# An encoder layer on one core: x^T from a second host layout, and the mean square by products with ones

## The chip, the core and the metric

The kernel runs on one core of a Trainium2 chip. The metric is the device time in microseconds (us) of one execution; the median of three runs is taken. The core's engines work side by side, each through its own list of instructions in order: TensorE (PE, matrix products into PSUM; PEld are its weight loads), VectorE (DVE), ScalarE (ACT), GpSimd (POOL) and SyncE (SP), which issues the DMA transfers. They wait for each other by semaphores.

## The reference

One layer of an encoder with 256 tokens and 2048 features, in float32. What bears on the change is the first norm and the first projections:

```python
def rms_norm(x, w):
    y = xf * lax.rsqrt(jnp.mean(xf * xf, axis=-1, keepdims=True) + EPS)
    return y * w
h = rms_norm(x, norm_mix_pre[l])
proj = jnp.einsum('bsd,dc->bsc', h, w_in[l])      # 2048 -> 10240 columns
qa, ka, va, qn, kn, vn, gates = jnp.split(proj, split_at, axis=-1)
```

Then follow two attention branches (qa and ka with rotary embedding), sigmoid gates, an output projection with post-norm and residual, and an MLP with 8192 hidden features.

## The kernel before

All 256 tokens are handled at once. Every product is made from operands in two float32r parts (high and low, whose sum is the float32 value). Weights come in chunks of four 128-row tiles by 512 columns (1 MB), each by one load on SP's queue; ACT casts the high part (line 115) and DVE subtracts it for the low part (line 116). Raw, high and low chunks have three buffers each. A group `wgroup` makes 512 output columns: 16 tiles k of the contraction in four chunks, four blocks b of 128 columns, each in its own PSUM bank, and per (b, k) a pair of products: the high weights on 512 columns (line 191: high and low part of the activations) and the low weights on 256 (line 192). The first group, qa_p, goes k by k in its first chunk and block by block in the others. Then come ka_p and, by `agroup`, va_p.

The activations hT are x^T times the gain g_pre, in two parts. x is loaded in four blocks of 512 features for all tokens (the first in two halves, with the first chunk's weights, one load per k, between them). `x_parts(i)` transposes block i on PE, two transposes per k (line 268), ACT takes the high part out of PSUM (line 273) and DVE the low part (line 274). `prelude(ch)` is traced ahead of chunk ch: x_parts(0) and (1) at chunk 0, (2) and (3) at chunks 1 and 2; the squares x_squares(0) at chunk 2, (1) to (3) at chunk 3.

The norm's scale is applied behind the products. `x_squares` squares on ACT and accumulates per token (line 345). `postlude`, traced in the last chunk behind block 0, calls `row_scales`: a reduction on DVE (line 300), then (mean + eps)^-0.5 with POOL's power (line 88), then `along_tokens`, which spreads the scale over all partitions by products with a tile of ones (rxb_p, line 78), and the multiplication of the cosine and sine tables by it (lines 304, 305). The rotary step of the evacuation of qa_p needs these tables, but the PSUM banks come free before it.

The order on each engine is planned by a list scheduler from the order in which the instructions are traced and from a simulated timeline; `issue_after` adds single constraints. The same x is loaded again for the residual, much later.

Of the kernel before, what the change touches and what calls it, by code (L numbers as in the profile page):

```python
# [11 lines left out]
F32 = mybir.dt.float32  # L12
F32R = mybir.dt.float32r
AF = mybir.ActivationFunctionType
ALU = mybir.AluOpType
# [23 lines left out]
def encoder_layer(ctx: ExitStack, tc: tile.TileContext, a, out):  # L39
# [32 lines left out]
    def along_tokens(r, b, name):  # L72
        """r [P tokens, token tile] as a row of all tokens, on all partitions."""
        ps = bank(f"{name}_p")
        for t in range(2):
            dg = t1k(f"{name}_d{t}")
            nc.vector.tensor_scalar_mul(dg[:, :P], ident, r[:, t : t + 1])
            nc.tensor.matmul(ps[:, t * P : (t + 1) * P], ones, dg[:, :P], start=True, stop=True)
        nc.scalar.copy(b, ps[:, :T])

    def inv_rms(ss, n, name, r=None):
        """(ss / n + eps) ** -0.5, per partition."""
        w = ss.shape[1]
        ms_ = small(w, f"{name}_m")
        nc.vector.tensor_scalar(ms_, ss, 1.0 / n, EPS, op0=ALU.mult, op1=ALU.add)  # L85
        if r is None:
            r = small(w, f"{name}_r")
        nc.gpsimd.tensor_tensor(r, ms_, expo[:, :w], op=ALU.pow)
        return r

# [1 line left out]
    last_load = [None]  # L92

    def load(src, k0, nk, c0, cw, name):
        """Rows k0*128.. of a weight: [P, nk, cw]."""
        raw = wp.tile([P, nk, cw], F32, tag="raw", name=f"{name}_w")
        view = src[k0 * P : (k0 + nk) * P, c0 : c0 + cw].rearrange("(k p) c -> p k c", p=P)
        last_load[0] = nc.sync.dma_start(raw, view).ins
        return raw

    def split(raw, name, pieces=2, after=()):
        """Two float32r parts whose sum is raw. after[s] are instructions that go ahead of piece s."""
        _, nk, cw = raw.shape
        hi = wp.tile([P, nk, cw], F32R, tag="hi", name=f"{name}_h")
        lo = wp.tile([P, nk, cw], F32R, tag="lo", name=f"{name}_l")
        for s in range(pieces):
            part = (
                (slice(None), slice(s * nk // pieces, (s + 1) * nk // pieces))
                if nk > 1
                else (slice(None), slice(None), slice(s * cw // pieces, (s + 1) * cw // pieces))  # L110
            )
            with ExitStack() as order:
                for ins in after[s] if after else ():
                    order.enter_context(tc.issue_after(ins))
                nc.scalar.copy(hi[part], raw[part])  # L115
                nc.vector.tensor_sub(lo[part], raw[part], hi[part].bitcast(F32))  # L116
        return hi, lo
# [3 lines left out]

# [1 line left out]
    g_pre = const.tile([P, KD], F32, name="g_pre")  # L123
# [6 lines left out]
    nc.gpsimd.memset(ones, 1.0)  # L130
    x = a["x"]
    xv = x.rearrange("(t p) c -> p t c", p=P)
    xp = []
    first = []
    for i in range(4):
        xt = page([P, 2, 512], F32, f"x_{i}")
        xi = xv[:, :, i * 512 : (i + 1) * 512]
        xp.append(xt)
        if i == 0:
            raw = wp.tile([P, 4, 512], F32, tag="raw", name="first0_w")  # L140
            view = a["w_in"][: 4 * P, QA : QA + 512].rearrange("(k p) c -> p k c", p=P)
            for h in range(2):
                cs = slice(h * 256, (h + 1) * 256)
                nc.sync.dma_start(xt[:, :, cs], xi[:, :, cs])
                for k in range(h * 2, h * 2 + 2):
                    nc.sync.dma_start(raw[:, k], view[:, k])
            first.append(raw)
        else:
            nc.sync.dma_start(xt, xi)
            if i < 3:  # L150
                first.append(load(a["w_in"], i * 4, 4, QA, 512, f"first{i}"))
    g_mlp = const.tile([P, KD], F32, name="g_mlp")
# [19 lines left out]
    def advance(n):  # L172
        """Trace the next n stages of the attention heads that wait for their turn, and one chore."""
        if chores:
            with tc.issue_after(last_load[0]):
                chores.pop(0)()
        for _ in range(n):
            if pending:
                g = pending.pop(0)
                if next(g, None):  # L180
                    pending.append(g)

    def wgroup(src, c0, act, nk, evac, name, first=(), hook=None, mid=None, after={}, k_first=False, inner=None):
        """out^T of 512 columns: weights stationary. act(k) is [P, hi 256 | lo 256]."""
        ps = [bank(f"{name}_p{b}", True) for b in range(4)]
# [34 lines left out]
    def agroup(src, c0, stat, nk, evac, name, tail=1, between=None):  # L220
        """out of 512 columns: activations stationary. stat(k, t) is (hi, lo) of [P, 128].
        The last ``tail`` chunks go token tile by token tile; between(i) may trace instructions
        ahead of the i-th of the second tile's products there and returns the last of them."""
        ps = [bank(f"{name}_p{t}", True) for t in range(2)]
# [26 lines left out]
    def halves(ps, name):  # L251
        """The sum of the two halves of a bank, in SBUF."""
        r = t1k(f"{name}_r")
# [4 lines left out]

# [1 line left out]
    hT = [page([P, 2, 512], F32R, f"hT{i}") for i in range(8)]  # L260

    def x_parts(i):
        """The transpose of four tiles of x times the gain, in two parts [P, hi | lo]."""
        acts = []
        for k in range(i * 4, i * 4 + 4):
            pt = bank(f"hT_t{k}")
            for t in range(2):
                nc.tensor.transpose(
                    pt[:, t * P : (t + 1) * P], xp[i][:, t, (k % 4) * P : (k % 4 + 1) * P], ident
                )  # L270
            d = hT[k // 2][:, k % 2]
            g = g_pre[:, k : k + 1]
            acts.append(nc.scalar.activation(d[:, :T], pt[:, :T], AF.Copy, scale=g).ins)
            nc.vector.scalar_tensor_tensor(
                d[:, T:], pt[:, :T], g, d[:, :T].bitcast(F32), op0=ALU.mult, op1=ALU.subtract
            )

        return acts
# [16 lines left out]

    ssx = const.tile([P, 8], F32, name="ssx")

    def row_scales():
        sx = small(2, "sx")
        nc.vector.tensor_reduce(sx, ssx.rearrange("p (t h) -> p t h", h=4), axis=AX.X, op=ALU.add)  # L300
        inv_rms(sx, D, "rx", rx)
        along_tokens(rx, rxb, "rxb")
# [16 lines left out]

    # Position bias: row (h, i) of rpbp holds the bias of row offset i - 3 at column offsets  # L320
    # -63..63. Each is written 64 times at a pitch of 127 and read at a pitch of 126.
    def skew_write(h):
# [18 lines left out]

    def x_squares(i):
        for t in range(2):
            j = junk512("jx0").rearrange("p a b -> p (a b)")
            nc.scalar.activation(
                j, xp[i][:, t], AF.Square, accum_out=ssx[:, t * 4 + i : t * 4 + i + 1]
            )

    def postlude():
# [15 lines left out]

# [1 line left out]
    oT = {}  # L367
# [6 lines left out]
    def product3(ps, stat, s_at, mov, m_at, start, stop):  # L374
        """ps (+)= stat^T @ mov, each given in two parts."""
        for i, (sp, mp) in enumerate(((0, 0), (0, 1), (1, 0))):
# [42 lines left out]
    def p_transposed(p, name):  # L419
        """[P queries, (t, keys)] -> [P keys, (key tile, queries)]"""  # L420
        pt = bank(f"{name}_pt")
# [171 lines left out]

# [1 line left out]
    mT = []  # L595
# [26 lines left out]

# [1 line left out]
    def mstat(k, t):  # L624
# [9 lines left out]
    for t in range(2):  # L634
        for h in range(2):
            nc.sync.dma_start(
                x2[t * 2 + h], x[t * P : (t + 1) * P, h * 1024 : (h + 1) * 1024]
            )
# [77 lines left out]

# [1 line left out]
    def first_up_inner(k):  # L718
# [103 lines left out]
def _host_arrays(inputs):  # L822
    f = {k: np.ascontiguousarray(v) for k, v in inputs.items()}
    arr = {
        "x": f["x"][0],
        "w_in": f["w_in"][0],
        "w_branch_a": f["w_branch_a"][0],
# [12 lines left out]
        "lam_k2": f["lam_k2"],  # L840
        # row offsets -3..3 are the ones that four rows reach
        "rpbp": np.pad(f["na_rpb"][0][:, 4:11], ((0, 0), (0, 0), (48, 48))),
# [30 lines left out]
```

## Time and profile before

| what | us |
|---|---|
| median of three runs | 1397.35 |
| lowest and highest run | 1396.53, 1397.74 |
| span of the profiled execution | 1394.5 |
| PE busy | 1374.6 |
| DVE busy | 835.8 |
| ACT busy | 668.7 |

The profiled execution is one run of the same program, from its first to its last instruction; a run's time holds some 3 us around that. Line numbers are those of the kernel before. In a timeline row stand the start, the duration and, in brackets, how long the engine had been idle and what ended that; "x4" merges four instructions that follow each other. Matmul ends are modelled, so the distance between starts tells the pace. A float32 product or transpose counts as one or two matmul rows.

### The profile page before, as it was taken

What the parts mean: (1) busy time and instruction counts of PE and PEld (TensorE: products, weight loads), DVE (VectorE), ACT (ScalarE), POOL (GpSimd) and SP (SyncE); (2) the same over time, 40 slices, a digit from 0 to 9 for tenths busy, and PEclk for the clock granted to TensorE, in tenths of its full rate; (3) what the DMA queues carried; (4) which work ended last, traced back from release to release, by engine and by line L of the source; (5) the groups of instructions that cost most, each with busy time, mean ns of one, the idle gap of its engine ahead of it and who ended that gap; (6) DMA issues with size and microseconds to landing.
All of it is one profiled execution on the core that took longest, in us unless ns stands there. A gap on an engine that the chain in (4) does not pass through costs nothing.

```text
span 1394.5 us, 17896 instructions
## 1 busy us (share of the span) xinstructions
PE 1374.6 (99%) x7240; PEld 1177.8 (84%) x7240; DVE 835.8 (60%) x1155; ACT 668.7 (48%) x1023; POOL 7.9 (1%) x19
## 2 busy tenths in 40 slices
PE   7999999999999999999899999999999999999997
PEld 6888888888888888888788888888888888888886
DVE  6868866676656565654755555555575554444445
ACT  7554554545444445543744444444464543334332
POOL 0000000000000000000000000000000000000000
PEclk9999999999999999999999999999999999999999
DMA  9674755564555555675455565656555556555551
GB/s 317 202 214 154 202 177 173 171 191 155 165 205 182 203 181 183 203 279 184 149 182 181 182 193 170 211 170 200 189 196 185 203 186 227 195 187 205 181 199 73
DMA packets 117490, 265.16 MB, mean 190 GB/s; under 512 B 15008, under 2 KB 16288, under 8 KB 109216
## 3 DMA queue, kind: packets, MB, share of 16 engines
q1 hardware_dynamic: 117264, 264.03, 57.3%
q8 instruction: 56, 0.92, 0.3%
q14 instruction: 26, 0.21, 0.0%
q10 hardware_dynamic: 144, 0.01, 0.0%
HBM read 261.92 MB, written 3.92 MB: 191 GB/s over the span
## 4 chain that ended last, share of the span: by engine, by line
PE 98%; DVE 1%; DMA 0%; ACT 0%; SPq 0%; issue 0%; DVEq 0%; POOLq 0%; POOL 0%; ACTq 0%
PE u_p L191 17%; PE u_p L192 9%; PE acc L779 8%; PE acc L778 8%; PE acc L777 8%; PE gb_p L191 4%; PE ga_p L191 4%; PE qa_p L191 2%; PE gb_p L192 2%; PE ga_p L192 2%; PE ka_p L191 2%; PE qn_p L191 2%; PE bb_p L191 2%; PE ba_p L191 2%; PE kn_p L191 2%; PE y_p L229 2%
## 5 line engine op out<-in xcount | busy, mean ns | idle before, releaser
L191 PE MATMUL u_p<-h2T,u_h 128*128 128x512 f32 x1024 | 359.9, 398 | 0.5 <-DVE r_m L85 0.5
L192 PE MATMUL u_p<-h2T,u_l 128*128 128x256 f32 x1024 | 284.3, 280 | 0.0
L116 DVE TENSOR_TENSOR d_l<-d_w,d_h 128x1024 fp32r<-128x1024 f32 x128 | 151.1, 1221 | 164.2 <-ACT d_h L115 163.7
L116 DVE TENSOR_TENSOR u_l<-u_w,u_h 128x1024 fp32r<-128x1024 f32 x128 | 151.1, 1222 | 146.0 <-ACT u_h L115 144.7
L191 PEld LDWEIGHTS u_p<-h2T,u_h 128*128 128x128 f32 x1024 | 192.0, 189 | 45.5 <-DVE r_m L85 0.9
L115 ACT CAST d_h<-d_w 128x1024 fp32r<-128x1024 f32 x128 | 128.3, 1052 | 191.1 <-PE acc L779 187.5
L778 PE MATMUL acc<-d_l,uh 128*128 128x512 f32 x512 | 199.0, 389 | 0.0
L779 PE MATMUL acc<-d_h,ul 128*128 128x512 f32 x512 | 198.9, 389 | 0.0
L777 PE MATMUL acc<-d_h,uh 128*128 128x512 f32 x512 | 198.2, 389 | 0.0
L192 PEld LDWEIGHTS u_p<-h2T,u_l 128*128 128x128 f32 x1024 | 193.8, 189 | 1.3
L115 ACT CAST u_h<-u_w 128x1024 fp32r<-128x1024 f32 x128 | 128.0, 1049 | 123.9 <-PE u_p L191 62.5
L778 PEld LDWEIGHTS acc<-d_l,uh 128*128 128x128 f32 x512 | 96.1, 188 | 20.1
L777 PEld LDWEIGHTS acc<-d_h,uh 128*128 128x128 f32 x512 | 96.1, 188 | 20.0
L779 PEld LDWEIGHTS acc<-d_h,ul 128*128 128x128 f32 x512 | 96.1, 188 | 19.8
L191 PE MATMUL gb_p<-hT,gb_h 128*128 128x512 f32 x256 | 90.4, 398 | 0.0
L191 PE MATMUL ga_p<-hT,ga_h 128*128 128x512 f32 x256 | 90.0, 397 | 0.0
L192 PE MATMUL gb_p<-hT,gb_l 128*128 128x256 f32 x256 | 71.4, 281 | 0.0
L192 PE MATMUL ga_p<-hT,ga_l 128*128 128x256 f32 x256 | 70.3, 280 | 0.0
L191 PEld LDWEIGHTS gb_p<-hT,gb_h 128*128 128x128 f32 x256 | 47.9, 188 | 11.5
L116 DVE TENSOR_TENSOR gb_l<-gb_w,gb_h 128x1024 fp32r<-128x1024 f32 x32 | 37.8, 1221 | 31.1 <-ACT gb_h L115 31.1
L191 PEld LDWEIGHTS ga_p<-hT,ga_h 128*128 128x128 f32 x256 | 47.4, 188 | 10.5
L116 DVE TENSOR_TENSOR y_l<-y_w,y_h 128x1024 fp32r<-128x1024 f32 x32 | 37.9, 1222 | 27.8 <-ACT y_h L115 27.8
(213 smaller groups left out, 2348.1 us busy)
## 6 DMA issues: line engine op xcount, KB each, us to landing
u_w<-in_w_up SPq DMA_DIRECT2D x64, 1024.0 KB, 5.4
d_w<-in_w_down SPq DMA_DIRECT2D x64, 1024.0 KB, 4.9
ga_w<-in_w_in SPq DMA_DIRECT2D x16, 1024.0 KB, 5.2
gb_w<-in_w_in SPq DMA_DIRECT2D x16, 1024.0 KB, 5.2
y_w<-in_w_out SPq DMA_DIRECT2D x16, 1024.0 KB, 5.1
ka_w<-in_w_in SPq DMA_DIRECT2D x8, 1024.0 KB, 6.1
va_w<-in_w_in SPq DMA_DIRECT2D x8, 1024.0 KB, 5.2
qn_w<-in_w_in SPq DMA_DIRECT2D x8, 1024.0 KB, 5.1
```

The costliest lines, as they stand in the source:

```text
L115: nc.scalar.copy(hi[part], raw[part])
L116: nc.vector.tensor_sub(lo[part], raw[part], hi[part].bitcast(F32))
L191: nc.tensor.matmul(ps[b], hi[:, k % 4, cs], mv, start=(k == 0), stop=False)
L192: nc.tensor.matmul(ps[b][:, :T], lo[:, k % 4, cs], mv[:, :T], start=False, stop=(k == nk - 1))
L229: nc.tensor.matmul(ps[t], sh, hi[:, k % 4], start=(k == 0), stop=False)
L777: nc.tensor.matmul(acc[t][c], uh[:, k % 4, ts_], hi[:, 0, cs], start=(k == 0), stop=False)
L778: nc.tensor.matmul(acc[t][c], uh[:, k % 4, ts_], lo[:, 0, cs], start=False, stop=False)
L779: nc.tensor.matmul(acc[t][c], ul[:, k % 4, ts_], hi[:, 0, cs], start=False, stop=(k == NK - 1))
```

## The change

The host stores x a second time, transposed and tiled: xT is [128 features, 16 tiles k, 256 tokens]. The kernel loads xT instead of x at the start, in the order in which tiles are used, all on SP's queue, with weight loads between: the first weight tile, x^T of k = 0, the second weight tile, x^T of k = 1 to 3, two more weight tiles, then for each of the next two chunks the block of x^T and the weights in two halves, then the last block of x^T. `x_parts` reads these tiles from SBUF and has no transposes. `x_squares` squares a whole block [128, 4, 256] on ACT and adds its four tiles on DVE into ssx [128, 256], a sum per partition and token. `row_scales` makes two products of ssx with one column of ones, which sum over the partitions, and goes on as before from PSUM. (Removed comments are left out.)

```diff
-    for i in range(4):
-        xt = page([P, 2, 512], F32, f"x_{i}")
-        ...
+    xT = [page([P, 4, T], F32, f"xT{i}") for i in range(4)]
+    first = [wp.tile([P, 4, 512], F32, tag="raw", name=f"first{i}_w") for i in range(3)]
+    fv = [ ... ]
+    nc.sync.dma_start(first[0][:, 0], fv[0][:, 0])
+    nc.sync.dma_start(xT[0][:, 0:1], a["xT"][:, 0:1])
+    nc.sync.dma_start(first[0][:, 1], fv[0][:, 1])
+    nc.sync.dma_start(xT[0][:, 1:4], a["xT"][:, 1:4])
+    for k in range(2, 4):
+        nc.sync.dma_start(first[0][:, k], fv[0][:, k])
+    for i in range(1, 3):
+        nc.sync.dma_start(xT[i], a["xT"][:, i * 4 : i * 4 + 4])
+        for h in range(2):
+            nc.sync.dma_start(first[i][:, h * 2 : h * 2 + 2], fv[i][:, h * 2 : h * 2 + 2])
+    nc.sync.dma_start(xT[3], a["xT"][:, 12:16])
...
     def x_parts(i):
-            pt = bank(f"hT_t{k}")
-            for t in range(2):
-                nc.tensor.transpose(
-                    pt[:, t * P : (t + 1) * P], xp[i][:, t, (k % 4) * P : (k % 4 + 1) * P], ident
-                )
+            src = xT[i][:, k % 4]
-            acts.append(nc.scalar.activation(d[:, :T], pt[:, :T], AF.Copy, scale=g).ins)
+            acts.append(nc.scalar.activation(d[:, :T], src, AF.Copy, scale=g).ins)
-                d[:, T:], pt[:, :T], g, d[:, :T].bitcast(F32), op0=ALU.mult, op1=ALU.subtract
+                d[:, T:], src, g, d[:, :T].bitcast(F32), op0=ALU.mult, op1=ALU.subtract
...
-    ssx = const.tile([P, 8], F32, name="ssx")
+    ssx = const.tile([P, T], F32, name="ssx")
+    def x_squares(i):
+        sq = page([P, 4, T], F32, f"xsq{i}")
+        nc.scalar.activation(sq, xT[i], AF.Square)
+        nc.vector.tensor_add(sq[:, 0:2], sq[:, 0:2], sq[:, 2:4])
+        if i == 0:
+            nc.vector.tensor_add(ssx, sq[:, 0], sq[:, 1])
+        else:
+            nc.vector.tensor_add(sq[:, 0], sq[:, 0], sq[:, 1])
+            nc.vector.tensor_add(ssx, ssx, sq[:, 0])
     def row_scales():
-        sx = small(2, "sx")
-        nc.vector.tensor_reduce(sx, ssx.rearrange("p (t h) -> p t h", h=4), axis=AX.X, op=ALU.add)
-        inv_rms(sx, D, "rx", rx)
+        ps = bank("rx_p")
+        for t in range(2):
+            nc.tensor.matmul(
+                ps[:, t : t + 1], ssx[:, t * P : (t + 1) * P], ones[:, :1], start=True, stop=True
+            )
+        inv_rms(ps[:, :2], D, "rx", rx)
...
-    def x_squares(i):
-        for t in range(2):
-            j = junk512("jx0").rearrange("p a b -> p (a b)")
-            nc.scalar.activation(
-                j, xp[i][:, t], AF.Square, accum_out=ssx[:, t * 4 + i : t * 4 + i + 1]
-            )
```

## Rows read from the trace of the kernel before

**Rows 1.** The page: busy time of the engines; the chain by engine.

```profile
PE 1374.6 (99%) x7240; PEld 1177.8 (84%) x7240; DVE 835.8 (60%) x1155; ACT 668.7 (48%) x1023; POOL 7.9 (1%) x19
...
PE 98%; DVE 1%; DMA 0%; ACT 0%; SPq 0%; issue 0%; DVEq 0%; POOLq 0%; POOL 0%; ACTq 0%
```

**Rows 2.** PE's waits, whole span: total us, times, longest.

```profile
PE hT_t L268 <- DMA x<-in_x: 6.0, 2, 3.9
PE h2T_t L664 <- DVE x L657: 3.2, 1, 3.2
```

**Rows 3.** The chain in order of time: start, us, what.

```profile
9.41 0.79 PE qa_p L191
...
12.33 0.97 PE hT_t L268 x6
...
25.78 0.66 PE hT_t L268 x6
...
31.76 0.44 PE rxb_p L78 x4
...
36.74 0.23 PE ka_p L191
```

**Rows 4.** Timeline of PE, two pairs early and two later.

```profile
10.85 0.63 PE L191 MATMUL qa_p<-hT,qa_h 128*128 128x512 f32 x1
...
11.49 0.63 PE L191 MATMUL qa_p<-hT,qa_h 128*128 128x512 f32 x1
...
15.12 0.40 PE L191 MATMUL qa_p<-hT,qa_h 128*128 128x512 f32 x1
...
15.48 0.40 PE L191 MATMUL qa_p<-hT,qa_h 128*128 128x512 f32 x1
```

**Rows 5.** Busy by stretch; after POOL: granted clock, DMA share, GB/s.

```profile
0.00:10.00 10.00, 2.79 (x10) 1.93 (x10) 1.83 (x4) 4.76 (x11) 0.88 (x8) 1.00 0.72 243
5.00:6.00 1.00, 0.03 (x1) 0.00 (x0) 0.27 (x1) 0.62 (x1) 0.00 (x0) 1.00 0.67 214
10.00:11.00 1.00, 1.00 (x5) 0.90 (x4) 1.00 (x3) 1.00 (x3) 0.00 (x0) 1.00 1.06 408
14.00:15.00 1.00, 1.00 (x9) 0.89 (x7) 0.69 (x1) 1.00 (x2) 0.00 (x0) 1.00 1.04 387
```

**Rows 6.** Timeline of ACT.

```profile
5.08 0.62 ACT L115 CAST qa_h<-first_w 128x512 fp32r<-128x512 f32 x1 [2.61 <-DMA first_w<-in_w_in]
7.14 0.63 ACT L345 ACTIVATE jx<-x 128x512 f32<-128x512 f32 x1 [1.45 <-DMA x<-in_x]
...
8.38 1.54 ACT L273 ACTIVATE hT<-hT_t,g_pre 128x256 fp32r<-128x256 f32 x4
```

**Rows 7.** Timeline of DVE.

```profile
8.87 1.66 DVE L274 SCALAR_TENSOR_TENSOR hT<-hT_t,g_pre,hT 128x256 fp32r<-128x256 f32 x4 [2.45 <-ACT hT L273]
10.46 1.90 DVE L116 TENSOR_TENSOR qa_l<-first_w,qa_h 128x512 fp32r<-128x512 f32 x3
...
29.32 1.22 DVE L116 TENSOR_TENSOR ka_l<-ka_w,ka_h 128x1024 fp32r<-128x1024 f32 x1
...
35.76 0.42 DVE L385 TENSOR_TENSOR rope_u<-rope_s,sinT 64x256 f32<-64x256 f32 x1
...
49.23 2.36 DVE L116 TENSOR_TENSOR ka_l<-ka_w,ka_h 128x1024 fp32r<-128x1024 f32 x2 [1.83 <-ACT ka_h L115]
```

**Rows 8.** DVE alone by stretch: length, busy time, granted clock, DMA share, GB/s.

```profile
8.87:20.90 12.03, 9.99 (x16) 1.00 1.05 384
20.90:30.95 10.05, 9.29 (x21) 1.00 0.98 334
30.95:51.65 20.70, 17.05 (x33) 1.00 0.49 156
```

**Rows 9.** DMA issues: times, KB each, median us to landing.

```profile
first_w<-in_w_in SPq DMA_DIRECT2D x2, 1024.0 KB, 10.1
...
g_pre<-in_g_mix_pre ACTq DMA_DIRECT2D x1, 8.0 KB, 2.4
```

More of the change, by code (lines that the diff above doesn't have):

```diff
@@ L130, in encoder_layer @@
     nc.gpsimd.memset(ones, 1.0)
[L131 to L134, printed above, removed]
-    for i in range(4):
-        xt = page([P, 2, 512], F32, f"x_{i}")
[L137 to L151, printed above, removed]
+    xT = [page([P, 4, T], F32, f"xT{i}") for i in range(4)]
+    first = [wp.tile([P, 4, 512], F32, tag="raw", name=f"first{i}_w") for i in range(3)]
+    fv = [
+        a["w_in"][i * 4 * P : (i + 1) * 4 * P, QA : QA + 512].rearrange("(k p) c -> p k c", p=P)
+        for i in range(3)
+    ]
+    nc.sync.dma_start(first[0][:, 0], fv[0][:, 0])
[9 more added lines that the diff above has]
+    nc.sync.dma_start(xT[3], a["xT"][:, 12:16])
     g_mlp = const.tile([P, KD], F32, name="g_mlp")
@@ L636, in encoder_layer @@
             nc.sync.dma_start(
-                x2[t * 2 + h], x[t * P : (t + 1) * P, h * 1024 : (h + 1) * 1024]
+                x2[t * 2 + h], a["x"][t * P : (t + 1) * P, h * 1024 : (h + 1) * 1024]
             )
@@ L825, in _host_arrays @@
         "x": f["x"][0],
+        "xT": f["x"][0].T.reshape(KD, P, T).transpose(1, 0, 2),
         "w_in": f["w_in"][0],
```

## The prediction

> **What bounds the kernel now.** I read the page first: PE is busy 99% of the span and carries 98% of the chain that ended last [rows 1]. So only two things can change the time: PE work on that chain, and the moments at which PE stands still. The waits of PE say where those are: 6.0 us for the loads of x in the first microseconds, 3.2 us far behind in the post-norm, and next to nothing else [rows 2]. The change touches the first of them alone. In order of time, the chain shows PE's real start: the first product of qa_p at 9.41, then products without a gap up to the next group, ka_p, at 36.74, with transposes among them [rows 3]. Behind 36.74 the change alters no instruction, so I compare the moment at which ka_p starts, and then ask whether what is won there can be kept.
>
> Three more readings of that stretch. The first products come 0.64 us apart per pair (a 512 and a 256 wide one), later ones 0.35 [rows 4]. The granted clock reads 1.00 in both [rows 5], the upper level of 2.4 GHz, but 512 columns in 0.43 us is the pace of the lower, 1.2 GHz; I go by the pace. It lasts from 9.41 to about 12.8, into the six transposes that take 0.97 instead of 0.66 [rows 3], and costs half of these 3.4 us, 1.7. ACT casts the first weights at 5.08, then stands until 7.14 for x and squares x ahead of the copies of x^T that PE needs (8.38) [rows 6]. And DVE is nearly full: 9.99 of 12.03 us, then 9.29 of 10.05, then 17.05 of 20.70 [rows 8].
>
> **The change part by part.** The sum is made on the span of 1394.5; the runs' median of 1397.35 lies 2.85 above it, and I take that distance as fixed.
>
> *Start.* The first weight tile (256 KB) now goes first. The first load before, x of the same size, ended PE's wait at 3.9 [rows 2], so the tile lands at 3.9. x^T of k=0 is second, with half of the bytes; the second load before was in ACT's hands at 5.08 [rows 6], so between 4.2 and 5.1; I take 4.5. Then ACT casts (0.62, to 4.55) and makes the high part of x^T (four in 1.54, so 0.38 [rows 6], to 4.95); DVE makes the low part of the weights (0.63, three in 1.90) and of x^T (0.42, four in 1.66) [rows 7], to 5.7 with a handover. First product at 5.75 instead of 9.41: 3.65 us won. Bounds: 3.9, and 2.4 if x^T comes as late as the second half of the first x block, which ACT awaited until 7.14 [rows 6], less what the casts then no longer take. The gain vector g_pre takes 2.4 us to land on ACT's queue [rows 9], done at about 3.1, under the weight load; without that cover each 0.1 us of it costs 0.1.
>
> *Transposes.* 32 leave PE; 8 ran before 9.41 and are in the start. The other 24 stood between products at 0.11 each at full pace (six in 0.66 [rows 3]): 2.65 won. Their PSUM banks are free too; nobody waited for these, so that counts as nothing.
>
> *Products with ones.* Two are added, on one moving column each. The trace has none so narrow. The nearest, rxb_p, is 0.44 for as many instructions on 128 columns [rows 3]; I take 0.2 lost, between 0.05 and 0.44. Removing the squares' accumulators saves ACT about eight pairs of 0.62 and adds four squares of 1024 columns at some 1.0 (as the cast of that size): ACT gains 1 us, off the path.
>
> *Slow pace.* Its 1.7 us move with the start. Nothing won; bounds below.
>
> So far 3.65 + 2.65 - 0.2 = 6.1 us.
>
> *Loads.* All issues stay on SP, 13 instead of 9, and x^T has as many bytes as x had. PE now asks earlier. With chunk 0 started at 5.75, its 16 pairs take 5.6 + 1.7, and chunk 1 is due at 13.05, its second half two pairs later, 13.75. By then 1.57 + 0.52 + 1.05 = 3.15 MB must have landed. Before, 2.43 MB were moved by 10.0 and 0.41 MB in each of the next microseconds [rows 5]: 11.8, and up to 13 since loads under way share the engines (a 1 MB load of this stretch took 10.1 us [rows 9]). From 12.4, a cast of 1.0 and a subtraction of 1.2 [rows 7] end at 14.6: PE waits 0.8, between 0 and 2.
>
> *DVE.* This is the hidden price. Each x_squares now puts adds on DVE: one of 512 elements (0.63) and two of 256 (0.40, the 0.42 of a rope operation [rows 7] less the overlap of successive ones), one less for the first: 4 x 0.63 + 7 x 0.40 = 5.3, less some 0.15 for the small reduction that goes, 5.15. The same engine makes the low part of every weight. Before, that of ka_p's first chunk was ready at 30.54 [rows 7] and PE came at 36.74: 6.2 ahead. Its fourth was ready at 51.6, PE (48 pairs on) at 53.5: 1.9 ahead. After: DVE starts at 4.55 rather than in earnest at 8.87. Up to ka_p's first chunk it has 0.63 + 9.99 + 9.29 [rows 8] + 5.15 = 25.1 us of work, so 29.7 with no gap, 31.0 with 1.3 us in which it must wait for chunk 1's data; PE is there at 36.74 - 5.3 = 31.4. Up to the fourth, 17.05 more: 48.0, against 48.2. DVE thus runs at PE's heels for 40 us, where it had up to 6 us in hand. Every gap in DVE then shows on PE. Before it had 2.0 + 0.8 + 3.65 = 6.45 us of gaps between 8.87 and 51.65 [rows 8], of which 1.83 is one wait for a cast of ka_p's weights [rows 7]. I take 1.2 us of PE waits, between 0 (the spare gaps take the adds) and 3.6 (gaps behind chunk 1 come again).
>
> *The chain to the scales.* PE now holds a wait on DVE's last add, in front of the products of blocks 1 to 3 of chunk 3; behind it the power on POOL, two DVE operations, rxb_p and the cosine tables follow as before. The whole chain was covered: rxb_p ran at 31.76 with products on both sides [rows 3]. I count it at nothing; a late add costs what it is late.
>
> Sum: 6.1 - 0.8 - 1.2 = 4.1 us won; 1397.35 - 4.1 = 1393.2.
>
> **The rivals.**
>
> *Supply keeps up.* The adds fall into DVE's early gaps and chunk 1 is in time. For it: those gaps stand just where the first loads are awaited. Then 5.3 to 6.1 are kept: 1391.5.
>
> *DVE sets the pace.* The adds stand ahead of chunk 3's split in the program, so they may run ahead of it, and all the later gaps return: 3.6 us of waits instead of 1.2, 1.7 won: 1395.6. For it: the two sums above leave 0.2 to 0.4 us of slack in 40. Against it: DVE's order is planned and ka_p's splits can go first.
>
> *The slow pace lasts longer.* Before, PE had run eight transposes from 3.9 on; the pace rose 3.4 us after the first product, but 8.9 us after the first transpose [rows 2 to 4]. If the transposes helped to raise it, the low pace may last up to 8.9 us behind 5.75, half of 5.5 more: 2.7 us, of which 0.8 covers the wait for chunk 1. 2.2 won: 1395.1. The Trainium skill (TensorE: Matmul & The Clock Gate, "What's actually happening") has the lower clock as the default that activity lifts. By that rule the removed transposes are activity taken away. Their pace agrees, the granted clock of 1.00 does not show it.
>
> *The loads come late, so that the change does not bring an earlier supply.* The change cuts the first loads into smaller ones. If they moved at the 214 GB/s of 5 to 6 us [rows 5], 3.15 MB would take 14.7 us from their start at about 2, land at 16.7 and be split at 18.9: PE waits 5.1 instead of 0.8, DVE's lateness hides in that, 1.0 won: 1396.4. Against it: the stretch of 10 to 11 us moved 408 [rows 5]. The Trainium skill (DMA: Bandwidth & Descriptors, "Measured (HBM→SBUF, 128 partitions, SWDGE, issued from GpSimd)") asks for loads of 1 MiB and more. No row here shows small loads alone, and this rule speaks against the cut.
>
> *Slower: the products with ones block PE.* PE meets them after block 0 of chunk 3, near 26.5. If DVE does the last adds only behind the splits of ka_p's first two chunks (4.55 + 0.63 + 9.99 + 9.29, 2.4 for the second chunk, 5.15 and 1.3 make 33.3), and an estimated 1.7 us of power, copies and rxb_p follow before PE goes on, PE stands 8.5 us: 5.3 - 8.5 = 3.2 lost, 1400.6. It decides from 5.3 us of standing on. Against it: the adds come earlier in the program than those splits.
>
> **How the numbers follow.** Forecast as summed 0.47; supply keeps up 0.18; DVE sets the pace 0.20; slow pace 0.05; late loads 0.06; blocked by the ones 0.04. The forecast's own range, with the bounds of the waits and of the start, is 1392.2 to 1394.5. For 8 in 10 I reach down to 1391.0 (supply keeps up) and up to 1395.8 (DVE sets the pace, most of it); outside lie late loads, the block and the far ends. Under 0.2% (2.8 us) this kernel's measurement cannot be told from no change, so the line for faster is 1394.55: forecast and first rival, with a fourth of the DVE case, give 0.70; same 0.26; slower 0.04.
>
> **What would show it.** In the profile of after: no transposes in the first 30 us; the first qa_p product near 5.75 (over 7: the start was wrong); the first pairs at 0.64 for some 3.4 us; ka_p's first product near 32.6 (36.74 - 4.1); PE's waits naming DVE's low parts qa_l and ka_l, about 2 us in total. No such waits would mean that supply keeps up. A wait of PE on ssx over 1 us shows the chain exposed, a wait on a load past chunk 1 late loads. I am wrong at the root if ka_p starts 4 us earlier and the end does not follow: then some later stage was not bound by PE.

## The result, and the profile after

The kernel after takes 1399.45 us (median of 20 runs, 1398.02 to 1401.05), the kernel before on the same chip 1397.32 (20 runs, 1395.92 to 1398.25). The ratio is 1.0015, 95% interval [1.0009, 1.0022]: 2.1 us slower, where 4.1 us faster was forecast. The profiled spans say the same, 1396.4 against 1394.5. (A run lies 1.7 us above the span of the same execution, 1398.14 for 1396.4, and not 3; both profiles caught executions some 1 us faster than their median.) The difference is a little under the 2.8 us that the prediction set as its line for slower; it lies outside the range all the same, and the forecast had the wrong sign.

The waits of PE over the whole span (total us, times, longest) come first. They answer to [rows 2]:

```profile
PE qa_p L188 <- DVE hT L267: 6.3, 2, 5.4
PE h2T_t L663 <- DVE x L656: 3.2, 1, 3.2
PE rxb_p L78 <- DVE rxb_d L77: 3.0, 1, 3.0
PE ka_p L188 <- DVE rope_s L253: 1.2, 1, 1.2
```

The post-norm's 3.2 are unchanged. The start is there (5.4, with 0.9 more at k = 1), but two waits are new, 3.0 and 1.2 us: PE waits for the scale of the norm, then for an addition that empties a bank. No wait names the low parts of weights (qa_l, ka_l), which the prediction had watched.

The timeline of PE after says where (start, duration, what, in brackets the idle time before it and what ended that):

```profile
5.39 0.79 PE L188 MATMUL qa_p<-hT,qa_h 128*128 128x512 f32 x1 [5.39 <-DVE hT L267]
...
6.84 0.63 PE L188 MATMUL qa_p<-hT,qa_h 128*128 128x512 f32 x1
...
9.24 2.08 PE L188 MATMUL qa_p<-hT,qa_h 128*128 128x512 f32 x4 [0.92 <-DVE hT L267]
...
32.53 0.50 PE L304 MATMUL rx_p<-ones,ssx 128*128 128x1 f32 x4
35.98 0.71 PE L78 MATMUL rxb_p<-rxb_d,ones 128*128 128x128 f32 x4 [2.95 <-DVE rxb_d L77]
37.88 0.76 PE L188 MATMUL ka_p<-hT,ka_h 128*128 128x512 f32 x1 [1.18 <-DVE rope_s L253]
...
38.65 0.63 PE L188 MATMUL ka_p<-hT,ka_h 128*128 128x512 f32 x1
...
41.21 0.44 PE L188 MATMUL ka_p<-hT,ka_h 128*128 128x512 f32 x1
```

and ka_p's first product in the same view of the kernel before:

```profile
36.58 0.39 PE L191 MATMUL ka_p<-hT,ka_h 128*128 128x512 f32 x1
```

(The chain of [rows 3] counts it only from the end of the product ahead of it, 36.74.) The first product is 4.0 us earlier (5.39 for 9.41), and qa_p makes way at 32.53, 4.0 us ahead of the 36.58 at which ka_p began before. Up to there the change brings what it promised. Then the two products with ones, rxb_p and two waits stand alone on PE, which they didn't before: rxb_p ran at 31.76 between products. ka_p starts at 37.88, 1.3 us later than before, and its first five pairs come 0.64 apart instead of 0.35. So ka_p takes 23.85 us up to va_p (37.88 to 61.73) where it took 22.31 (36.58 to 58.89), and va_p is 2.84 late.

About 1 us of that comes back far behind, and by chance: u_p starts 2.78 late (676.74 for 673.96), the first product of acc 1.76 late (1038.98 for 1037.22). u_p begins at half pace in both kernels, behind the post-norm's wait, but for 2.8 us after and 4.5 before (PE's busy time, granted clock, DMA share, GB/s; after, then before):

```profile
676.74:679.55 2.81, 2.81 (x9) 0.50 0.00 0
673.96:678.45 4.49, 4.49 (x15) 0.50 0.00 0
```

Half of the difference is 0.8 us. The length of this stretch is not the kernel's: in two profiles of one and the same program (e6 and e11, below) the granted clock reads 0.50 there for 3.3 and 6.8 us.

Why these waits: the timeline of DVE, which works in order.

```profile
28.15 2.35 DVE L116 TENSOR_TENSOR ka_l<-ka_w,ka_h 128x1024 fp32r<-128x1024 f32 x2
30.43 0.41 DVE L299 TENSOR_TENSOR ssx<-ssx,xsq 128x256 f32<-128x256 f32 x1
31.69 2.36 DVE L116 TENSOR_TENSOR ka_l<-ka_w,ka_h 128x1024 fp32r<-128x1024 f32 x2 [0.85 <-ACT ka_h L115]
33.96 0.15 DVE L85 TENSOR_SCALAR rx_m<-rx_p 128x2 f32<-128x2 f32 x1
...
34.51 1.22 DVE L116 TENSOR_TENSOR ka_l<-ka_w,ka_h 128x1024 fp32r<-128x1024 f32 x1
35.65 0.47 DVE L77 TENSOR_SCALAR rxb_d<-ident,rx 128x128 f32<-128x128 f32 x2
...
36.18 1.22 DVE L116 TENSOR_TENSOR ka_l<-ka_w,ka_h 128x1024 fp32r<-128x1024 f32 x1
37.31 0.41 DVE L253 TENSOR_TENSOR rope_s<-qa_p,rope_r 128x256 f32<-128x256 f32 x1
```

Every step of the chain stands behind a low part of ka_p's weights that PE doesn't need yet (the products with ones, PE's step, behind the whole of qa_p): the last addition (30.43) behind 28.15, rx_m (33.96) behind 31.69, rxb_d (35.65) behind 34.51, and the addition that empties the first bank of qa_p (37.31) behind 36.18. The engine is full all that time:

```profile
7.92:20.70 12.78, 12.60 (x22) 1.00 1.04 394
20.70:31.00 10.30, 9.89 (x18) 1.00 0.84 269
```

(stretch, its length, DVE busy with its instructions, granted clock, DMA share, GB/s; compare [rows 8].) The planner put the products with ones last in PE's list of qa_p and the low parts ahead of the scale's steps on DVE. In the kernel before the reduction ran at 21.19 and rxb_d 9 us ahead of rxb_p; the first bank of qa_p was emptied at 35.72, which is only 0.86 us ahead of ka_p's first product:

```profile
22.63 0.47 DVE L77 TENSOR_SCALAR rxb_d<-ident,rx 128x128 f32<-128x128 f32 x2
...
35.30 0.42 DVE L256 TENSOR_TENSOR rope_s<-qa_p,rope_r 128x256 f32<-128x256 f32 x1 [0.50 <-ACT rope_r L254]
```

### The profile page after: what moved, and what is told of

The parts are those of the page before. It is cut to its first block, busy times and chain, and to the rows that moved or that the text cites. A ratio compares the mean times of both kernels' runs of the same rounds, so it can differ in the third digit from the quotient of the medians.

```text
span 1396.4 us, 17850 instructions
## 1 busy us (share of the span) xinstructions
PE 1372.7 (98%) x7212; PEld 1175.8 (84%) x7212; DVE 839.9 (60%) x1165; ACT 668.0 (48%) x1011; POOL 7.9 (1%) x19
## 4 chain that ended last, share of the span: by engine, by line
PE 96%; DMA 2%; DVE 1%; ACT 0%; issue 0%; SPq 0%; DVEq 0%; POOLq 0%; POOL 0%; ACTq 0%
PE u_p L188 17%; PE u_p L189 9%; PE acc L778 8%; PE acc L776 8%; PE acc L777 8%; PE gb_p L188 4%; PE ga_p L188 4%; PE ka_p L188 2%; PE gb_p L189 2%; PE ga_p L189 2%; PE qn_p L188 2%; PE kn_p L188 2%; PE bb_p L188 2%; PE ba_p L188 2%; PE y_p L228 2%; PE y_p L226 2%
## 5 line engine op out<-in xcount | busy, mean ns | idle before, releaser
L116 DVE TENSOR_TENSOR gb_l<-gb_w,gb_h 128x1024 fp32r<-128x1024 f32 x32 | 37.7, 1221 | 31.1 <-ACT gb_h L115 31.1
```

## The experiments

Theory A: the eleven additions, and the place that the planner gives the scale's steps and the emptying of the banks behind them on a full DVE, cost the gain. The rivals, by the letters that the expectations use: B, the longer half pace at the start (the transposes that PE ran ahead of it are gone); C, DVE has too much work in whatever order; D, the place of the products with ones in PE's order; E, the loads of x^T or the half pace, and not the squares; F, the loads hold each other up on SP's queue.

The runs were made on several chips. Where two kernels from different chips are compared, each is set against the kernel before on its own chip.

### Idle products first (e1_warm)

```diff
     nc.gpsimd.memset(ones, 1.0)
+    wps = bank("warm_p")
+    for _ in range(18):
+        nc.tensor.matmul(wps[:, :P], ones, ones, start=True, stop=True)
```

> The changed kernel with 18 idle float32 products of the ones tile (128 x 128) put on PE ahead of the first real product, into a bank that nobody reads; nothing else changes. Theory A (the scale chain on DVE sets the start of ka_p): the products of qa_p run at the pace of 0.35 us per pair sooner and end near 29 to 31 instead of 32.5, but rxb_p still waits for DVE, ka_p still starts within 1 us of 37.9, and the time stays within 1 us of 1399.4. Rival B (the longer stretch at half pace, some 2 us more than before, is what made the change slower): ka_p starts 2 to 4 us earlier and the time falls to 1395.5 to 1397.5.

Measured: 1399.68, ratio to the kernel before 1.0018 [1.0009, 1.0027], no gain on the kernel after. The timeline of PE shows the early products at full pace, 0.35 per pair instead of 0.64, and what became of it:

```profile
7.79 0.47 PE L191 MATMUL qa_p<-hT,qa_h 128*128 128x512 f32 x1
...
8.22 0.40 PE L191 MATMUL qa_p<-hT,qa_h 128*128 128x512 f32 x1
...
8.57 0.39 PE L191 MATMUL qa_p<-hT,qa_h 128*128 128x512 f32 x1
...
31.49 0.50 PE L307 MATMUL rx_p<-ones,ssx 128*128 128x1 f32 x4
35.79 1.22 PE L78 MATMUL rxb_p<-rxb_d,ones 128*128 128x128 f32 x4 [3.79 <-DVE rxb_d L77]
37.68 0.77 PE L191 MATMUL ka_p<-hT,ka_h 128*128 128x512 f32 x1 [0.67 <-DVE rope_s L256]
```

The idle products ended 2.4 us later than the first real one could have started, yet qa_p is done 1 us earlier. That is lost in a longer wait for rxb_d (3.79), and ka_p starts at 37.68 for 37.88. So B falls: DVE's chain, not PE's pace, sets when ka_p starts.

### The chain in front (e2_chain)

Two orders on DVE, no change of work: the low parts of qa_p's fourth chunk behind the last addition (qa_after is {3: that addition}), those of ka_p's chunks 1 to 3 behind rxb_d (last_rxd).

```diff
-    head = dict(first=first, hook=prelude, mid=postlude, k_first=True)
+    head = dict(first=first, hook=prelude, mid=postlude, k_first=True, after=qa_after)
...
-            wgroup(w_in, kc + off, hmov, KD, kev(kT), f"k{nm}")
+            wgroup(w_in, kc + off, hmov, KD, kev(kT), f"k{nm}", **(dict(after={c: (last_rxd[0],) for c in range(1, 4)}) if nm == "a0" else {}))
```

> The changed kernel with two constraints of issue order on DVE alone: the low part of chunk 3 of qa_p behind the last add into ssx, and those of ka_p's chunks 1 to 3 behind the two operations that spread the scale (rxb_d). No work is added or taken away. Theory A (the chain of scales is late because DVE makes low parts of ka_p in between): rxb_p waits under 1 us instead of 2.95, ka_p starts at 33.5 to 36 instead of 37.9, without a second stretch at half pace or a shorter one, and the time falls by 2 to 6 us, to 1393.5 to 1397.5. Rival B (half pace at the start): no change in ka_p's start beyond 1 us, 1399. Rival C (DVE simply has too much work, in whatever order): PE waits for low parts of ka_p instead, time 1398 to 1400.

Measured: 1396.49, ratio 0.9994 [0.9985, 1.0003], 2.6 us under the kernel after. PE's timeline:

```profile
26.28 0.50 PE L308 MATMUL rx_p<-ones,ssx 128*128 128x1 f32 x4
31.92 0.71 PE L80 MATMUL rxb_p<-rxb_d,ones 128*128 128x128 f32 x4
34.78 0.50 PE L190 MATMUL ka_p<-hT,ka_h 128*128 128x512 f32 x1 [2.16 <-DVE rope_s L255]
```

rx_p and rxb_p have moved between products and wait for nothing. What is late next is the bank: rope_s ran at 34.31, behind 2.35 us of ka_l, and PE waits 2.16; behind that wait the granted clock falls again (0.50 from 35.3 to 38.7).

### The additions left out (e3_noadd)

Ten of the eleven additions are left out, so the scales are not those of the reference; all else stays.

```diff
-        nc.vector.tensor_add(sq[:, 0:2], sq[:, 0:2], sq[:, 2:4])
-        if i == 0:
+        if i == 3:
             nc.vector.tensor_add(ssx, sq[:, 0], sq[:, 1])
-        else:
-            nc.vector.tensor_add(sq[:, 0], sq[:, 0], sq[:, 1])
-            nc.vector.tensor_add(ssx, ssx, sq[:, 0])
```

> The changed kernel without ten of the eleven adds of squares: ssx is the sum of two tiles of the last block only, so the scales are not those of the reference. The squares on ACT, the products with ones and all that follows stay. Theories A and C (the 5 us of adds on DVE are the cause, as a late chain or as work): ka_p starts 3 to 5 us earlier, 33 to 35, and the time falls to 1393 to 1396.5. A rival D (it is the place of the products with ones in PE's order, not the adds): rxb_p still waits 2 us or more and the time stays above 1398.

Measured: 1394.71, ratio 0.9983 [0.9974, 0.9991], 4.4 us under the kernel after. rxb_p waits for nothing (32.68) though the products with ones stay, so D falls; ka_p starts at 34.33 after a wait of 1.04 for rope_s. By the starts of the rows of after, the ten additions take DVE 4.4 us (four of 0.60, six of 0.34), and the end moves by about as much.

### The same additions in the kernel before (e8_before_adds)

The kernel before with eleven additions of the same sizes from its x tiles, and its own reduction queued behind the last of them.

```diff
+        nc.vector.tensor_add(dm[:, 0:2], xp[i][:, :, :T], xp[i][:, :, T:])
+        if i == 0:
+            last_add[0] = nc.vector.tensor_add(dsum, dm[:, 0], dm[:, 1]).ins
+        else:
+            nc.vector.tensor_add(dm[:, 0], dm[:, 0], dm[:, 1])
+            last_add[0] = nc.vector.tensor_add(dsum, dsum, dm[:, 0]).ins
...
+        with tc.issue_after(last_add[0]):
+            nc.vector.tensor_reduce(
+                sx, ssx.rearrange("p (t h) -> p t h", h=4), axis=AX.X, op=ALU.add
+            )
```

> The kernel before with one part of the change's cost: DVE makes eleven adds of the same shapes as the change has (on x, into a tile that nobody reads), and the reduction for the scales is queued behind the last of them. Transposes, loads and products are those of before. Theory A: the 5 us on DVE make the scales and the banks late here too; PE waits 2 to 6 us at rxb_p or at ka_p's start, and the time rises to 1399 to 1404. Rival: DVE's spare time (6 us ahead at ka_p) takes them, time within 1 us of 1397.

Measured: 1404.06, ratio 1.0050 [1.0035, 1.0065], 6.8 us slower than before. With all transposes and loads as they were, the same picture appears. DVE and PE:

```profile
38.50 0.15 DVE L303 TENSOR_REDUCE sx<-ssx 128x2 f32<-128x8 f32 x1
38.57 1.22 DVE L116 TENSOR_TENSOR ka_l<-ka_w,ka_h 128x1024 fp32r<-128x1024 f32 x1
...
40.77 0.48 DVE L77 TENSOR_SCALAR rxb_d<-ident,rx 128x128 f32<-128x128 f32 x2 [0.15 <-POOL rx L88]
```

```profile
41.20 1.19 PE L78 MATMUL rxb_p<-rxb_d,ones 128*128 128x128 f32 x4 [5.17 <-DVE rxb_d L77]
42.04 0.77 PE L191 MATMUL ka_p<-hT,ka_h 128*128 128x512 f32 x1
```

So the additions suffice for the wait. That they cost more here than in the kernel after would fit with a later start of the chain (the first addition runs at 25.31, for 20.72), but no run tells that apart.

### x^T alone, squares the old way (e4_oldsq, e5_oldsq_late)

The host's x^T for the products and, for the squares, x loaded as well behind it (2 MB more); in e5 the head's constants are also moved behind the evacuation of qa_p.

```diff
+    for i in range(4):
+        nc.sync.dma_start(xp[i], xv[:, :, i * 512 : (i + 1) * 512])
...
+            nc.scalar.activation(j, xp[i][:, t], AF.Square, accum_out=ssx[:, t * 4 + i : t * 4 + i + 1])
```

> One part of the change alone: x^T from the second layout with its order of loads and no transposes, but the mean square as before, on ACT from x with accumulators, and without products of ssx with ones. For this x is loaded as well (2 MB more, behind the last block of x^T), which delays the later weight loads by about 5 us. Theory A: the first product comes at 5.4, ka_p starts at 32 to 34, and the time is 3 to 5 us under that of before, 1392.5 to 1394.5. Rival E (the change is slower for its loads or for the half pace at the start, not for the squares): the time is within 2 us of 1399.4. If the extra loads bind, PE waits in chunk 3 of qa_p or in ka_p for a load, and the gain is smaller by that wait.

> As the run with the squares from x (x^T without transposes, mean square on ACT with accumulators, x loaded as well), but the constants of the heads (the products of lq on DVE) are traced in the last chunk of ka_p, behind the evacuations of qa_p, so that DVE does not stand in front of those for the loads of lq, which the extra loads of x had pushed to 36.8 us. Theory A: ka_p starts at 33 to 36 instead of 40.3, and the time is 1394 to 1397. Rival F (the loads on SP's queue themselves hold the start up: each load waits until the one issued eight before it has landed): PE waits for a weight load or for the cosine tables instead, and the time stays above 1398.

Measured: e4 1401.38, ratio 1.0028 [1.0016, 1.0039]; e5 1398.78, ratio 1.0009 [1.0000, 1.0019]. Both expectations were missed, and the pair says little about the part alone, because the extra loads disturb what they stand beside. In e4 one small operation on DVE held up everything behind it:

```profile
36.91 0.42 DVE L313 TENSOR_TENSOR lv<-lq 128x256 f32<-128x256 f32 x1 [1.61 <-DMA lq<-in_lam_k]
...
39.85 0.41 DVE L257 TENSOR_TENSOR rope_s<-qa_p,rope_r 128x256 f32<-128x256 f32 x1
```

The small loads of lq, behind the extra x on SP's queue, landed at 36.8, and PE waited 4.1 for the rope_s behind them. The queue's part of F is in the trace: no load left before the one issued eight before it had landed (the first lq left at 26.43, qa_w had landed at 26.37). PE's waits, though, name neither a weight load nor the tables.

In e5 the lq operation is out of the way, but the wait at k = 1 is 4.0 (0.92 in the kernel after; 0 to 2.2 in profiles of other kernels), and sx comes at 25.21 after DVE stood 3.17. The wait at k = 1 comes from the order on ACT, which is the same in e4. The high part of the weights of k = 1 stands behind the x^T of k = 4 to 7, for whose load ACT stood 1.49; in the kernel after it stands ahead of them (8.59 and 10.14):

```profile
10.01 1.70 ACT L272 ACTIVATE hT<-xT,g_pre 128x256 fp32r<-128x256 f32 x4 [1.49 <-DMA xT<-in_xT]
11.62 3.54 ACT L115 CAST qa_h<-first_w 128x512 fp32r<-128x512 f32 x5
```

What is left from the two: the first product still starts at 5.3 (e4) and 5.4 (e5). And in e5, which has no additions, the bank is late all the same: rope_s (37.92) stands behind 2.4 us of ka_l, and PE waits 2.04 for it. Rival E is not settled by them; the next three runs settle it.

### An order that keeps the gain (e6_order, e11_order_again, and e9_order_before)

The kernel after with its work unaltered. qa_p's fourth chunk is split behind the last addition, as in e2. The copy and addition that empty a bank (`halves`) go ahead of the rotary steps and of ka_p's casts and low parts: two banks ahead of chunk 1, all four ahead of chunks 2 and 3. The rotary steps (collected in rests) and the head's constants (by the hook late) go behind them. e9 is the kernel before with the same order.

```diff
-        nc.scalar.copy(r, ps[:, T:])
+        act = nc.scalar.copy(r, ps[:, T:]).ins
...
-        nc.vector.tensor_add(s, ps[:, :T], r)
+        evacs.append((act, nc.vector.tensor_add(s, ps[:, :T], r).ins))
...
+            for f in rests:
+                with tc.issue_after(evacs[3][1]):
+                    f()
...
-            wgroup(w_in, kc + off, hmov, KD, kev(kT), f"k{nm}")
+            wgroup(w_in, kc + off, hmov, KD, kev(kT), f"k{nm}", hook=late if nm == "a0" else None, after={1: evacs[1], 2: evacs[3], 3: evacs[3]} if nm == "a0" else {})
```

> The whole change, its work unaltered, with orders on DVE and ACT: the low part of chunk 3 of qa_p behind the last add of squares; the four evacuations of qa_p's banks (copy and add) ahead of the rotary steps and ahead of the casts and low parts of ka_p's chunks 1 (two of them) and 2, 3 (all four); the constants of the heads later. Theory A (what the change wins at the start is lost because DVE's order lets PE wait for the scales and for free banks): ka_p starts at 32.5 to 34, within 1.5 us of the end of qa_p, no second stretch at half pace, time 1392 to 1395. Rival C (DVE has too much work in any order): PE waits for low parts of ka_p's chunks instead, in sum as long, and the time stays at 1396 or above.

> e6_order once more, beside the kernel before in its new order on the same chip, so that the two can be set against each other. Theory A: 1392.5 to 1393.3, some 4.4 us under e9_order_before. Rival: no more than 1 us under it.

> The kernel before with the hand-made order of e6_order (evacuations of qa_p's four banks ahead of the rotary steps and of the casts and low parts of ka_p's chunks 1 to 3, head constants later; the constraint on the adds has nothing to bind, as there are no adds). Theory A (the change is worth its start and its transposes, about 4 to 6 us, and the planner's order gave that away again): PE has no wait in this stretch of the kernel before, so the order alone brings nothing, 1396.5 to 1398, and e6's 4.4 us belong to the change. Rival (the order is better by itself and the change is worth nothing): 1393 to 1394.5 here too. If the constraints cost the kernel before something (squares or scales later), over 1398.

Measured: e6 1392.90, ratio 0.9968 [0.9958, 0.9978]; e11, the same kernel, 1392.63, ratio 0.9966 [0.9953, 0.9978]. Beside e11 on the same chip, e9 took 1397.91, ratio 1.0000 [0.9992, 1.0009]. The order by itself is worth nothing to the kernel before; with it the change is worth 4.4 to 5.1 us against before, and e11 lies 5.3 under e9. That is theory A. C falls, since the additions are all there, and so does E, since the loads and the half pace at the start are those of the kernel after. (The single profiles scatter around that: e11's span of 1391.8 is 2.7 under that of before and 5.2 under that of e9, 1397.0.) PE and then DVE of e11:

```profile
9.54 2.08 PE L188 MATMUL qa_p<-hT,qa_h 128*128 128x512 f32 x4 [0.93 <-DVE hT L269]
...
28.08 0.50 PE L309 MATMUL rx_p<-ones,ssx 128*128 128x1 f32 x4
33.25 0.61 PE L78 MATMUL rxb_p<-rxb_d,ones 128*128 128x128 f32 x4
33.61 0.47 PE L188 MATMUL ka_p<-hT,ka_h 128*128 128x512 f32 x1
```

```profile
28.53 2.35 DVE L116 TENSOR_TENSOR ka_l<-ka_w,ka_h 128x1024 fp32r<-128x1024 f32 x2
...
31.85 0.48 DVE L77 TENSOR_SCALAR rxb_d<-ident,rx 128x128 f32<-128x128 f32 x2 [0.90 <-POOL rx L88]
...
32.42 0.90 DVE L255 TENSOR_TENSOR rope_s<-qa_p,rope_r 128x256 f32<-128x256 f32 x2
33.84 2.36 DVE L116 TENSOR_TENSOR ka_l<-ka_w,ka_h 128x1024 fp32r<-128x1024 f32 x2 [0.52 <-ACT ka_h L115]
```

The start, the wait at k = 1 and the length of the half pace are those of the kernel after (the 9.54 row: four products in 2.08, as at 9.24 there). From 28 us on nothing stands: rx_p and rxb_p lie between products, the two additions that empty the first banks (32.42) come ahead of the next low parts, and ka_p follows without a wait at full pace, 4.3 us earlier than after. This kernel is faster than both.

### Two tries at the rest (e7_order_warm, e10_order_split)

e7 is e6 with ten of e1's idle products; e10 is e6 with x^T of k = 1 in a load of its own, ahead of the weights of k = 1.

```diff
     nc.sync.dma_start(xT[0][:, 0:1], a["xT"][:, 0:1])
+    nc.sync.dma_start(xT[0][:, 1:2], a["xT"][:, 1:2])
     nc.sync.dma_start(first[0][:, 1], fv[0][:, 1])
-    nc.sync.dma_start(xT[0][:, 1:4], a["xT"][:, 1:4])
+    nc.sync.dma_start(xT[0][:, 2:4], a["xT"][:, 2:4])
```

> The run before (orders on DVE and ACT) with ten idle products of the ones tile on PE ahead of the first real one, some 4.3 us from 1.2 on. In the run with 18 of them the pace rose about 5.5 us after the first. If the scale chain and the banks no longer bind, the shorter half pace counts now: 1 to 3.5 us less than without the idle products, 1389.5 to 1393. If DVE binds (rival C), no gain: within 1 us of the run without them, and PE's waits grow by what it comes earlier.

> e6_order with x^T of k=1 in a load of its own (128 KB, third in the queue, ahead of the weights of k=1). If PE's wait at k=1 (0.45 to 2.2 us from profile to profile) costs as it stands, its removal gives 0.3 to 1.5 us on e6_order: 1391.5 to 1392.6. If weights of k=1, which go one place later, end the wait instead, no difference: 1392.9.

Measured: e7 1391.94, ratio 0.9964 [0.9951, 0.9977]; e10 1393.25, ratio 0.9967 [0.9955, 0.9979]. Neither can be told from e6 and e11. In e10 the wait at k = 1 changes its name, but it isn't the load of the weights that ends it. ACT waits for the x^T of k = 2 and 3 first, and the high part of k = 1, whose weights had landed at 7.57, stands behind it (PE's wait; two rows of ACT's timeline):

```profile
PE qa_p L189 <- ACT qa_h L115: 1.2, 1, 1.2
...
8.27 0.91 ACT L269 ACTIVATE hT<-xT,g_pre 128x256 fp32r<-128x256 f32 x2 [2.66 <-DMA xT<-in_xT]
9.08 1.64 ACT L115 CAST qa_h<-first_w 128x512 fp32r<-128x512 f32 x3
```

So e10 doesn't show the start without that wait. Nor does e7 show what a shorter half pace is worth: its wait at k = 1 was 2.17, and behind it the granted clock fell again, to 0.50 from 10.7 to 14.1.

What a faster chunk 0 would be worth, e6 and e11 hint at: the two are one program. In e6's profile the pace rose 4.1 us after the first product, in e11's 8.5 after it, and still ka_p starts at 33.58 in one and 33.61 in the other: what e6 had won, it lost again in waits for ssx (0.5), qa_l (0.5) and rxb_d (0.8).

## Why the prediction was wrong

*What bounds the kernel, and where to look.* Right: the end moved with ka_p's start. But comparing only the moment at which ka_p starts missed that ka_p also has to find an emptied bank and PE at full pace.

*Start.* Right: 5.39 where 5.75 was forecast, 4.0 us won instead of 3.65. (Two more profiles with the loads of before have their first product at 8.78, e8, and 10.39, e9, so either figure is good to some 1 us.)

*Transposes.* Nothing contradicts their 2.65, though no run measured them alone. From 5.39 to 32.53 PE takes 27.14 us; less the wait of 0.92 that leaves 26.22 for the products of qa_p. Before, 9.41 to 36.58 less rxb_p (0.36 between the starts around it) and the transposes (2.65) is 24.16. The 2.06 left over agree with the next point.

*Slow pace.* Mis-sized. It was to move with the start, 3.4 us of it. In the profile after it lasts from 5.39 to about 14.0: 8.61 us, 7.68 of them busy, half of which is lost, 3.8 where 1.7 was counted. So 2.1 us more, near the 2.7 that the rival "slow pace lasts longer" gave. As a cause of the result it is nearly nothing all the same: in e1, and in e6 beside e11, a shorter half pace is taken back by the waits that follow.

*Products with ones.* Two on one column take 0.50 together, above the upper bound of 0.44. They stood alone and had been counted at 0.2.

*Loads.* 0.8 was right in size by luck, for the place was wrong: no wait at chunk 1, but 0.92 at k = 1. ACT stood from 4.63 to 7.37 for x^T of k = 1 to 3, one load, with the high part of the weights of k = 1, landed at 5.3, behind it in its list. (The loads are 13 instead of 11, not of 9.) The rival of late loads didn't come. In the stretches that it spoke of:

```profile
5.40:9.00 3.60, 2.92 (x8) 1.00 0.98 339
9.00:14.00 5.00, 4.76 (x14) 1.00 1.03 393
```

(PE's busy time, granted clock, DMA share, GB/s.) The loads of these stretches moved 339 and 393 GB/s, not 214. The Trainium skill's rule (DMA: Bandwidth & Descriptors, "Measured (HBM→SBUF, 128 partitions, SWDGE, issued from GpSimd)") for loads of 1 MiB and more speaks against the cut. It was measured there on loads issued from GpSimd; these are SP's, and in this stretch the measured rates show no such loss.

*DVE.* The load was counted rightly (5.3 us of additions forecast, 4.8 by the starts of the rows; the low part of ka_p's first chunk is ready at 30.50, forecast 29.7 to 31.0; DVE has hardly a gap from 7.92 to 37.7), and that "DVE thus runs at PE's heels" was right. What follows from it was not: the 1.2 us of waits were to name qa_l and ka_l. They name rxb_d and rope_s, because the planner served the low parts first, and everything else on DVE became late.

**The step that failed: "The chain to the scales".** "The whole chain was covered", it says, and "I count it at nothing; a late add costs what it is late." The cover was the 9 us between rxb_d at 22.63 and rxb_p at 31.76 in the kernel before. After, the chain begins with additions that end at 30.84 and its next steps stand behind what is left of qa_p on PE (rx_p at 32.53), then on DVE behind 2.4 us of low parts, 1.2 and 1.2. Between the end of qa_p at 32.53 and the first product of ka_p at 37.88 lie 5.35 us: 0.50 for rx_p, 2.95 of wait, 0.72 for rxb_p, 1.18 of wait. 0.64 of that was in the sum. The other 4.7, and 1.5 for the pace that falls again while PE stands, are the forecast's miss. Together: 0.4 more at the start, 0.1 and 2.0 lost at k = 1 and by the slow pace, 1.2 not spent on low parts, 4.7 and 1.5 lost here, and 0.9 that came back, most of it by the chance at the start of u_p. That is 5.8 of the 6.0 between 4.1 won and 1.9 lost on the spans.

*The rival "products with ones block PE"* has the right kind of mechanism and result (1400.6 against 1399.45), for the right reason: additions behind the splits of ka_p. The place and the size differ. PE did not stand in front of rx_p near 26.5; the planner knew ssx to be late and put rx_p behind the whole of qa_p, so PE stood behind it, 4.1 us in place of 8.5. What spoke against it, that the additions come earlier in the program than those splits, is no reason with this planner: the last addition (30.43) ran behind low parts that are traced after it (28.15). The 0.04 that it got was far too little.

*The banks, passed over.* "Their PSUM banks are free too; nobody waited for these" considered only the transposes' banks. Those of qa_p are emptied by DVE, and ka_p's first product needs one. Its lead before, 0.86 us, was smaller than those that were weighed (6.2 and 1.9 for low parts, 9 for the scale), and a qa_p that ends 4.0 us earlier uses it up with or without additions. With the scale in time PE still waits for rope_s: 2.16 in e2, 1.04 in e3 without ten of the additions, 2.04 in e5 without any.

*What the change is worth* was near the sum: 4.1 forecast, 4.4 (e6) and 5.1 (e11) measured, once the order on DVE leaves the chain its place. That the figures are so close is in part luck: 2.1 us too little for the slow pace stand against 1.2 us for low parts that PE didn't wait for and 0.4 at the start.

## What to carry to other kernels

An engine that is 60% busy over the span may be full for 30 us in the stretch that is changed; then an added operation delays all that stands behind it by its own length, and the price appears where a delayed operation is due first, not at the one that was added. So list everything that the full engine does for the engine that sets the end, the emptying of banks and small chains included, with its lead time before the change, and set the added work, and what the other engine is to come earlier, against the smallest lead (here 0.86 us, beside 9 for the scale). Where a planner sets the order, don't argue from the order of the program: after the change, look for needed small operations that stand behind bulk work with a later due time, and fix these by hand before the change is given up.

## What the runs showed of the hardware

The granted clock of the first microseconds is not a reading. The trace of after holds its first clock record at 13.98 us, that of before at 12.85, e6 at 9.37 and e11 at 14.13, each of them 1.00, the upper level of 2.4 GHz, and each where the pace of PE rises. For the time ahead of it the views say 1.00, in after also for 0 to 5 us, when PE did nothing, while products go at 0.64 per pair from 5.39 on. So there the distance of starts tells the pace. In the second slow stretch of the same profile the clock reads 0.50, and pace and record agree (windows of PE: busy time, granted clock, DMA share, GB/s):

```profile
32.50:36.00 3.50, 0.55 (x7) 1.00 0.94 305
...
37.90:41.20 3.30, 3.30 (x10) 0.50 0.99 309
```

Behind 3.5 us in which PE was busy for 0.55, the pace was the lower level's, 1.2 GHz, for 3.3 us; from 41.21 on the pairs come some 0.35 apart again. By the Trainium skill (TensorE: Matmul & The Clock Gate, "What's actually happening") the lower clock is the default and activity lifts it; this row agrees. These waits of PE cost their length and 1.5 us more; waits that short had been summed at their length alone. Not every wait did: behind the 2.04 us of e5 the first pairs of ka_p come 0.35 apart (38.84, 39.19).

How soon the pace rises after the first product is not a property of the kernel: 3.4 us in the profile of before, 5.5 in e9, which starts alike, 8.6 after, and 4.1 and 8.5 in two profiles of the same program (e6 and e11). What decides it stays open.
